# A gated-delta recurrence inside a larger two-block network: one state tile per head with an identity half, and epilogues emitted in more, smaller steps

## The chip, the cores and the metric

One NeuronCore of a Trainium2 chip runs the whole program in one launch. The metric is the device time of one execution in microseconds. The kernel before took 4145.36 us, the median of three runs (4140.95 to 4150.91). All data are float32.

## The reference

The program is a chain of two blocks on one sequence of 1024 tokens with 1024 features. The change lies in the second layer of the first block, in its recurrent branch. What is computed there, cut to the part that matters:

```python
def wkv_scan(r, w, k, v, a, bb, s0, reverse):
    def step(s, inp):
        r_t, w_t, k_t, v_t, a_t, b_t = inp
        sa = jnp.einsum("bhvk,bhk->bhv", s, a_t)
        s = s * w_t[:, :, None, :] + sa[..., None] * b_t[:, :, None, :] + v_t[..., None] * k_t[:, :, None, :]
        return s, jnp.einsum("bhvk,bhk->bhv", s, r_t)
    ...
# rwkv_branch: 8 heads of 64, once forward and once backward (d = 0, 1)
    s_fin, o = wkv_scan(r_h, heads(decay), k_d, v_h, -kk, kk * a_h, init, reverse=(d == 1))
# then: o = outs[0] + outs[1], normalised per head, times lnx_g, plus lnx_b, plus bonus * v, times the gate g
```

A context of 256 tokens is scanned first and gives the states with which the 1024 tokens start. Beside the recurrence the layer has dense projections (`h @ in_o`), a 31-tap convolution with a layer norm (`conformer_branch`) and an output projection (`y @ w_out`). Before this layer come its even neighbour, after it two feed-forward layers, a token mixer with top-k attention and norms.

## The kernel before

**Chunks.** The scan is done in chunks of 64 tokens. Four chunks of a pair of heads in one direction make a *group*; there are 4 head pairs, 2 directions and 5 groups each (group 0 is the context), so 40 groups, numbered n = 0 to 39. Five groups of one pair and direction are a *unit* (u = 0 to 7). The two heads of a pair lie on partitions 0 to 63 and 64 to 127 (`H[0]`, `H[1]`).

**Three stages per group.** `s1` (L660) builds decayed keys, queries and the chunk's triangular matrices and stores them in DRAM (`d_rec`). When all five groups of a unit are there, `elim` (L716) inverts the triangular 32x32 blocks by elimination, one part of the columns on VectorE (tiles `elUV`, `elTV`), the other on GpSimd (`elUP`, `elTP`), reading `elM` from `d_rec` and writing `d_el`; the other stages take them from there as `Tc` (L748). `s2` (L744) then makes from them, in steps, for each chunk the transition matrix Q and an additive matrix C (L777 to 789) and walks the four chunks (L798 to 805): output `o = S q + C`, new state `S = decay * (Q S + S + C)`. The three terms of the state are three matmuls that accumulate in PSUM, two of them by the identity (`mm`, L804); the output has two (L801). Each works on 64 rows and 64 columns of the array, one set for each head. VectorE scales the sum by the decay into the next of four state tiles `SI` (L805).

**Epilogues.** When both directions of a quarter of a head pair are done, `finish` (L810) loads the two outputs (`fok`), adds them on GpSimd (L816), normalises per head with transposes through TensorE (L824, L829, L844) and stores `d_yc`. `cln` (L599) is the same for the convolution branch and stores `d_yd`. Smaller epilogues of the projections are `g` inside `fk` (norm of the keys: ScalarE squares `kq`, L520, TensorE sums them, L523) and `norm` (L535). They are generators that wait in two lists, `later[0]` (projection epilogues and `cln`) and `later[1]` (`finish`).

**The order.** The order on TensorE in this layer is written out by hand: matmuls of the recurrence and of the dense work go through `Pinned`, which keeps them in program order. The main loop (L903 to 932) takes for each n four quarters. In each it first issues dense units until a count that grows by 3.2 per n, later by 2.4, is reached (L908 to 912), then one step of `s1` for the newest groups, one step of `s2` for group m = n - 9, and one step of the walk over the chunks for group m - 1. Elimination of a unit is issued when n is a multiple of 5 (L920). After each dense unit `fin` (L885) appends ready epilogues and calls `tick` (L496), which takes each list's first epilogue one step on:

```python
        for l in later:
            while l and next(l[0],l) is l: l.pop(0)
```

`finish` is taken one step on at once when it is appended (`next` in L888), so its loads and its first two operations are issued, and its first matmul in the `tick` behind that. The last dense work is the output projection `outp` (L854), in four batches; each is issued when the epilogues that it reads have been issued (`fins`, L868), and until then every quarter counts 0.25 of a unit without work. All other engines' instructions are placed by a scheduler which knows priorities: 500 for the recurrence, 200 for the elimination (`EPRIO`), 1000 for epilogues.

## Time and profile before

| | |
|---|---|
| median of three runs | 4145.36 us |
| the profiled execution | 4132.25 us, span of its instructions 4130.5 us |
| TensorE (PE) busy | 3639.1 us, 88% |
| VectorE (DVE) busy | 2384.2 us, 58% |
| ScalarE (ACT) busy | 1474.9 us, 36% |
| GpSimd (POOL) busy | 1370.3 us, 33% |
| TensorE weight loads | 3166.6 us, 77% |
| mean granted TensorE clock | 0.921 of full speed |

The layer with the recurrence runs from about 700 to 2010 us of the span; `s2` starts its first group at 928 us. In the stretch the page shows TensorE busy in six to nine tenths of each slice, where the stages behind it show nine tenths, and the granted clock moves between 0.58 and 1.00. A row of the trace names line, engine, operation and out<-in tiles; a float32 matmul stands there as two instructions.

### The profile page before, as it was taken

The numbers are of one execution on the slowest core, as the hardware profiler recorded it, in microseconds if no ns is written. First come the engines' busy times: TensorE is split into PE (matmuls) and PEld (weight loads), VectorE is DVE, ScalarE is ACT, GpSimd is POOL, SyncE is SP. The second block draws the span as 40 slices with busy tenths as digits, with TensorE's granted clock in tenths as the row PEclk, the third lists the DMA queues.
The fourth block names the chain that finished last, engine by engine and source line by source line (L and its number), as shares of the span: only waits on it lengthen the run. The fifth ranks groups of instructions, "written<-read, shape, count | busy, mean of one in ns | idle before, by whom it ended". The sixth has DMA issues, their size and how long they took to land.

```text
span 4130.5 us, 72373 instructions
## 1 busy us (share of the span) xinstructions
PE 3639.1 (88%) x28552; PEld 3166.6 (77%) x28552; DVE 2384.2 (58%) x4265; ACT 1474.9 (36%) x2581; POOL 1370.3 (33%) x2335
## 2 busy tenths in 40 slices
PE   8999988878786867768679999999999989999997
PEld 6889878767775866646479998876666658999885
DVE  4445331358636635736476665654788666666455
ACT  3233222444432534422232223443565333222333
POOL 3021122246526535624353331111343323333012
PEclk9999999888887887879789999999899999999998
DMA  5453564877675767644322214551231002221554
GB/s 209 154 176 121 166 223 149 258 223 223 212 223 177 225 192 231 188 121 127 112 97 83 84 67 163 179 170 60 75 113 42 21 31 94 78 84 53 205 186 160
DMA packets 422997, 594.52 MB, mean 144 GB/s; under 512 B 106590, under 2 KB 322400, under 8 KB 412928
## 3 DMA queue, kind: packets, MB, share of 16 engines
q1 hardware_dynamic: 422656, 589.88, 44.6%
q8 instruction: 225, 3.69, 0.4%
q14 instruction: 116, 0.95, 0.1%
HBM read 453.45 MB, written 136.07 MB: 143 GB/s over the span
## 4 chain that ended last, share of the span: by engine, by line
PE 58%; DMA 13%; DVE 10%; POOL 6%; issue 6%; ACT 5%; SPq 2%; POOLq 0%; DVEq 0%; ACTq 0%
PE ps L72 13%; PE ps L73 13%; PE ps L74 13%; PE ps L21 10%; DMA wr<-in_f_w 2%; PE ps L1262 2%; PE ps L1250 1%; DVE elUV L738 1%; POOL elTP L737 1%; POOL elUP L738 1%; DVE elTV L737 1%; DMA d_ok<-O 1%; PE ps L1260 1%; DMA raw<-in_in_e 1%; DMA d_xh<-hls 1%
## 5 line engine op out<-in xcount | busy, mean ns | idle before, releaser
L21 PE MATMUL ps<-xq,hi 128*128 128x256 f32 x1632 | 329.4, 302 | 0.0
L72 PE MATMUL ps<-B,ffC 128*128 128x256 f32 x1056 | 298.7, 283 | 5.5 <-DVE ffC L88 2.9
L73 PE MATMUL ps<-B,ffC 128*128 128x256 f32 x1056 | 298.0, 282 | 3.6 <-DVE B L88 3.6
L74 PE MATMUL ps<-B,ffC 128*128 128x256 f32 x1056 | 298.3, 282 | 0.0
L21 PEld LDWEIGHTS ps<-xq,hi 128*128 128x128 f32 x1632 | 280.5, 210 | 3.2 <-issue 2.7
L73 PE MATMUL ps<-w,g 128*128 128x512 f32 x680 | 270.5, 398 | 13.3 <-DVE w L88 12.9
L74 PE MATMUL ps<-w,g 128*128 128x512 f32 x680 | 267.7, 394 | 0.0
L21 PE MATMUL ps<-xq,lo 128*128 128x256 f32 x816 | 258.1, 316 | 1.7 <-DMA xq<-d_xh 1.7
L88 DVE TENSOR_TENSOR w<-wr,w 128x1024 fp32r<-128x1024 f32 x132 | 172.2, 1305 | 138.4 <-ACT w L88 138.0
L72 PE MATMUL ps<-h,lo 128*128 128x320 f32 (+2 forms) x768 | 242.4, 317 | 2.5 <-DVE lo L67 1.7
L73 PE MATMUL ps<-h,hi 128*128 128x320 f32 (+2 forms) x768 | 239.4, 312 | 1.0 <-DVE h L262 1.0
L72 PE MATMUL ps<-w,g 128*128 128x512 f32 x680 | 233.4, 393 | 7.7 <-ACT w L88 4.4
L74 PE MATMUL ps<-h,hi 128*128 128x320 f32 (+2 forms) x768 | 238.9, 311 | 0.0
L67 DVE TENSOR_TENSOR lo<-raw,hi 128x1024 fp32r<-128x1024 f32 (+1 forms) x128 | 159.8, 1249 | 116.1 <-ACT hi L66 115.8
L997 POOL TENSOR_TENSOR ffraw<-ffraw 128x512 f32<-128x512 f32 x44 | 60.1, 1365 | 484.0 <-DVE A L88 484.0
L72 PE MATMUL ps<-B,A 128*128 128x256 f32 x704 | 201.5, 286 | 19.4 <-DVE A L88 18.0
L72 PE MATMUL ps<-B,S 128*128 128x256 f32 x704 | 203.1, 289 | 13.9 <-DVE S L88 13.9
L88 ACT CAST w<-wr 128x1024 fp32r<-128x1024 f32 x132 | 138.6, 1050 | 194.8 <-DMA wr<-in_f_w 111.4
L72 PEld LDWEIGHTS ps<-B,ffC 128*128 128x128 f32 x1056 | 200.0, 189 | 6.4 <-ACT B L88 3.3
L73 PE MATMUL ps<-B,S 128*128 128x256 f32 x704 | 202.6, 288 | 0.2
L73 PEld LDWEIGHTS ps<-B,ffC 128*128 128x128 f32 x1056 | 199.6, 189 | 4.0 <-DVE B L88 4.0
L73 PE MATMUL ps<-B,A 128*128 128x256 f32 x704 | 201.0, 286 | 1.8 <-DVE B L88 1.8
(487 smaller groups left out, 11173.8 us busy)
## 6 DMA issues: line engine op xcount, KB each, us to landing
xq<-d_xh SPq DMA_DIRECT2D x148, 512.0 KB
wr<-in_f_w SPq DMA_DIRECT2D x132, 512.0 KB
ffraw<-in_f_w SPq DMA_DIRECT2D x44, 1024.0 KB
d_rec<-R SPq DMA_DIRECT2D x32, 1024.0 KB
Q<-d_rec SPq DMA_DIRECT2D x32, 1024.0 KB
raw<-in_in_e SPq DMA_DIRECT2D x48, 512.0 KB
d_gg<-ffs SPq DMA_DIRECT2D x88, 256.0 KB
gr<-d_gg SPq DMA_DIRECT2D x44, 384.0 KB
```

Source lines behind the costliest of these rows:

```text
L21: def matmul(s,*a,**k): return s.pin(s.t.matmul(*a,**k))
L67: nc.vector.tensor_tensor(lo[:,:n],raw[:,:n],hi[:,:n],op=ALU.subtract)
L72: first=t.matmul(ps,lt[1],rt[0],start=start,stop=False)
L73: t.matmul(ps,lt[0],rt[1],start=False,stop=False)
L74: t.matmul(ps,lt[0],rt[0],start=False,stop=stop)
L88: s.nc.scalar.copy(hi,src); s.nc.vector.tensor_tensor(lo,src,hi,op=ALU.subtract)
L737: e.tensor_tensor(t,bc(M[:,sr,x:x+1],[80,ns,nj]),bc(U[:,x:x+1,jr],[80,ns,nj]),op=ALU.mult)
L738: e.tensor_tensor(U[:,sr,jr],U[:,sr,jr],t,op=ALU.add)
L997: nc.gpsimd.tensor_tensor(r[:,1],r[:,1],r[:,0],op=ALU.add)
L1250: p=k.ps("at"); nc.tensor.matmul(p[:,:m],q[r,h//2],kT[r,h//2,c0:c0+m],start=True,stop=True)
L1260: for c in range(m): nc.tensor.transpose(p[:,128*c:128*c+128],s[:,128*(c0+c):128*(c0+c)+128],ident)
L1262: for c in range(b+1): nc.tensor.matmul(po3[r,h//2],VT[:,c,64*h:64*h+64],pT[:,c],start=c==0,stop=c==b)
```

## The change

The state tile of each head now is 128 rows high: 64 rows of state and 64 rows of identity, kept in place (two tiles `SI` of [128, 2, 64] in turn, L650 after the change). Q and C no longer are two matrices: one matmul of full width (128 rows, 128 columns) per head and chunk gives both halves of a matrix `Q0` or `Q1`, and the identity that was added by its own matmul is added once by VectorE on the way out of PSUM. A step of the walk then has one matmul of 128 rows and 64 columns per head for the output and one for the state, in place of two and three. VectorE scales the state in two instructions, one per head, where it was one; the copy of `pk` (L765) moves from VectorE to ScalarE; the copies of C leave ScalarE. `finish` is appended without its first step, has an extra `yield` between its loads and its first operations and another ahead of its last matmuls; `g` of `fk` begins with a `yield`, with two buffers of `kq` and `rT`; `cln` has a list of its own; `tick` takes up to two entries of the first list one step on and one of each other list. `outp` counts 6 units for its first batch where it counted 4. The elimination's priority rises from 200 to 600.

```diff
-EPRIO=200
+EPRIO=600
...
-    later=([],[]); fins=set()
+    later=([],[],[]); fins=set()
     def tick():
-        for l in later:
-            while l and next(l[0],l) is l: l.pop(0)
+        for l,m in zip(later,(2,1,1)):
+            j=0
+            while j<m and j<len(l):
+                if next(l[j],l) is l: l.pop(j)
+                else: j+=1
...
-            q=F.tile([128,256],F32,tag="kq",name="kq"+nm)
+            q=F.tile([128,256],F32,tag="kq",bufs=2,name="kq"+nm)
             nc.scalar.activation(q,y,AF.Square,scale=V('k_k')[:,i:i+1])
             def g():
+                yield
...
-                for t in (n//2-4,n//2-3): later[0].append(cln(t))
+                for t in (n//2-4,n//2-3): later[2].append(cln(t))
...
-    NS=4
-    SI=[P.tile([128,64],F32,name="SI%d"%j) for j in range(NS)]
+    NS=2
+    SI=[P.tile([128,2,64],F32,name="SI%d"%j) for j in range(NS)]
+    for j in range(NS):
+        nc.vector.tensor_copy(SI[j][64:128,0],ident[64:128,64:128]); nc.vector.tensor_copy(SI[j][0:64,1],ident[0:64,0:64])
...
-        KV=A0+1; nc.vector.tensor_copy(R[:,:,KV],pk)
+        KV=A0+1; nc.scalar.copy(R[:,:,KV],pk)
...
-            for h in range(2): k.pe.matmul(p[H[h],c,:m],z[h][:,c,ks],R[:,c,T0+h:T0+h+5*m-4:5],start=True,stop=True)
-        nc.scalar.copy(q[:,:,0],p[:,:,0])
-        if isx: nc.vector.tensor_tensor(q[:,:,1],p[:,:,1],R[:,:,AR1],op=ALU.add)
-        p=k.ps("b1").rearrange("p (a b c) -> p a b c",a=4,b=2)
-        for c in range(4):
-            for h in range(2):
-                k.pe.matmul(p[H[h],c,0],R[:,c,T0+h],z[h][:,c,vs],start=True,stop=True)
-                if isx: k.pe.matmul(p[H[h],c,1],z[h][:,c,vs],R[:,c,RS0+h],start=True,stop=True)
-        nc.scalar.copy(C[:,:,:m],p[:,:,:m])
+            for c in range(4): k.pe.matmul(p4[:,c,:m],z[h][:,c],R[:,c,T0+h:T0+h+5*m-4:5],start=True,stop=True)
+            nc.vector.tensor_tensor(q[:,:,0],p4[:,:,0],bc(ident[:,H[h]].unsqueeze(1),[128,4,64]),op=ALU.add)
+            if isx:
+                nc.vector.tensor_tensor(q[H[h],:,1],p4[H[h],:,1],R[H[h],:,AR1],op=ALU.add)
+                nc.scalar.copy(q[H[1-h],:,1],p4[H[1-h],:,1])
...
-                for h in range(2): mm((po3[H[h],c],si[H[h]],q[H[h],c,1]),(po3[H[h],c],I_(h),C[H[h],c,1]))
+                for h in range(2): k.pe.matmul(po3[H[h],c],si[:,h],Q[h][:,c,1],start=True,stop=True)
...
-                for h in range(2): mm((p[H[h]],q[H[h],c,0],si[H[h]]),(p[H[h]],I_(h),si[H[h]]),(p[H[h]],I_(h),C[H[h],c,0]))
-                nc.vector.tensor_scalar(nx,p,PC[:,c],None,op0=ALU.mult)
+                for h in range(2): k.pe.matmul(p[H[h]],Q[h][:,c,0],si[:,h],start=True,stop=True)
+                for h in range(2): nc.vector.tensor_scalar(nx[H[h],h],p[H[h]],PC[H[h],c],None,op0=ALU.mult)
...
     def finish(i,hf):
...
+        yield
+        nc.gpsimd.tensor_tensor(ok[:,0:3:2],ok[:,0:3:2],ok[:,1:4:2],op=ALU.add)
...
         nc.vector.tensor_tensor(dd,dd,bc(rs.unsqueeze(2),[128,4,64]),op=ALU.mult)
         yield
+        yield
...
-                yield 0.01+(n==0)*4
+                yield 0.01+(n==0)*6
...
-                later[1].append(finish(*ready.pop(0)[1:])); next(later[1][-1])
+                later[1].append(finish(*ready.pop(0)[1:]))
```

Over the whole program TensorE has 1440 matmuls fewer (23482 before, 22042 after), VectorE 268 instructions more, ScalarE 24 copies and 3 table loads more. GpSimd has 8 memsets more, the DMA issues are the same in number.

**Place 1, the walk.** TensorE's rows of one step of the walk, both heads (unit 4, group 3; `Q`, `C` and `SI` are the transition, the additive matrix and the state; the first and the last row are the products ahead of the step and behind it; a row stands for one head, the other head's rows read alike and are left out, so that of ten products five are shown). Before:

```order
L21 MATMUL ps1716_17750<-Z0_1_6190,Q4_4_17538 64x64
L21 MATMUL ps1717_17770<-Q4_3_17652,SI0_6197 64x64
L21 MATMUL ps1717_17770<-C4_3_17653,ident_61 64x64
...
L21 MATMUL ps1717_17770<-SI0_6197,Q4_3_17652 64x64
L21 MATMUL ps1717_17770<-SI0_6197,ident_61 64x64
L21 MATMUL ps1717_17770<-C4_3_17653,ident_61 64x64
...
L21 MATMUL ps1718_17791<-R6_3_17525,BKB6_3_17530 128x128
```

After the change, the same step (`Q0`, `Q1` are the matrices of the two heads, the first and the last row the products ahead of it and behind it):

```order
L21 MATMUL ps1726_17199<-Z0_1_6190,Q4_4_16867 64x64
L21 MATMUL ps1727_17219<-Q0_4_3_17130,SI0_6197 64x64
L21 MATMUL ps1727_17219<-Q1_4_3_17139,SI0_6197 64x64
L21 MATMUL ps1727_17219<-SI0_6197,Q0_4_3_17130 64x64
L21 MATMUL ps1727_17219<-SI0_6197,Q1_4_3_17139 64x64
L21 MATMUL ps1728_17235<-R6_3_16854,BKB6_3_16859 128x128
```

Ten matmuls of the step have become four, and none of them works on the identity.

**Place 2, an epilogue's first matmul.** TensorE between the last product of the walk whose output an epilogue reads (unit 3, group 1) and the epilogue's first matmul (`fok`, head pair 1, quarter 3; `xq` is dense work). Before:

```order
L21 MATMUL ps1523_15240<-SI3_6200,ident_61 64x64
L21 MATMUL ps1523_15240<-C3_1_15099,ident_61 64x64
L21 MATMUL ps1559_15517<-xq1563_15523,lo1549_15496 128x256
L21 MATMUL ps1559_15517<-xq1563_15523,hi1549_15495 128x256 x2
...
L21 MATMUL ps1573_15675<-lwc5_3_15290,W2r_5_14225 128x256 x2
L21 MATMUL ps1574_15715<-Tc3_3_15211,Q3_3_15207 32x32 x8
...
L21 MATMUL ps1574_15715<-TU0_6201,X3_3_15219 32x32 x8
L21 MATMUL ps1575_15735<-Q3_2_15480,SI1_6198 64x64
...
L21 MATMUL ps1575_15735<-C3_2_15481,ident_61 64x64
L824 MATMUL ps1569_15648<-fok1_3_15630,BD_6161 128x256
```

After the change:

```order
L21 MATMUL ps1524_14795<-SI1_6198,Q1_3_1_14722 64x64
L21 MATMUL ps1559_15043<-xq1563_15049,lo1549_15022 128x256
L21 MATMUL ps1559_15043<-xq1563_15049,hi1549_15021 128x256 x2
...
L21 MATMUL ps1571_15166<-lwc5_3_14828,W2r_5_13833 128x256 x2
L21 MATMUL ps1572_15206<-Tc3_3_14766,Q3_3_14762 32x32 x8
...
L21 MATMUL ps1560_15044<-xq1561_15045,lo1555_15034 128x256
...
L21 MATMUL ps1573_15226<-Q0_3_2_15095,SI0_6197 64x64
...
L21 MATMUL ps1560_15044<-xq1563_15049,lo1555_15034 128x256
L827 MATMUL ps1584_15370<-fok1_3_15155,BD_6161 128x256
```

The epilogue's first matmul stands 56 rows behind the product before, 24 dense matmuls among them, and 85 rows behind it after, 52 of them dense matmuls. Over the 16 epilogues there are 0 to 72 dense matmuls in between before, and 0 to 267 after; in the epilogues of head pairs 0 and 1 24 to 72 before and 52 to 267 after.

**Place 3, the stretch ahead of the output projection.** TensorE between the first product with the inverse (`Tc`) of group 4 and that of the next unit's group 0, on both sides of the first work of the output projection (`yo`). Before:

```order
L21 MATMUL ps1716_17750<-Tc4_4_17542,Q4_4_17538 32x32 x8
L21 MATMUL ps1716_17750<-Z0_0_6189,Q4_4_17538 64x64
...
L21 MATMUL ps1717_17770<-C4_3_17653,ident_61 64x64
L21 MATMUL ps1720_17824<-hi1699_17456,yo1_1691_17435 128x512
L21 MATMUL ps1720_17824<-lo1699_17457,yo0_1691_17434 128x512
L21 MATMUL ps1720_17824<-hi1699_17456,yo0_1691_17434 128x512
...
L21 MATMUL ps1732_17977<-lwc7_0_17789,W2r_7_17784 128x256 x2
L21 MATMUL ps1733_18017<-Tc5_0_17739,Q5_0_17735 32x32 x8
```

After the change:

```order
L21 MATMUL ps1726_17199<-Tc4_4_16871,Q4_4_16867 32x32 x8
L21 MATMUL ps1726_17199<-Z0_0_6189,Q4_4_16867 64x64
...
L21 MATMUL ps1732_17288<-Q4_4_16867,TU0_6203 128x128 x4
L21 MATMUL ps1727_17219<-Q0_4_3_17130,SI0_6197 64x64
...
L21 MATMUL ps1735_17329<-lwc7_0_17233,W2r_7_17228 128x256 x2
L21 MATMUL ps1736_17369<-Tc5_0_17188,Q5_0_17184 32x32 x8
```

Before, the output projection began between the two products, and 24 of its matmuls stood there; two groups ahead of it (unit 4, groups 2 and 3) had no dense work. Now there is none between them, it starts behind the second, and three groups (unit 4, groups 3 and 4, unit 5, group 0) have no dense work.

## Rows read from the trace of the kernel before

**Rows 1.** Page, busy time of each engine, and the clock over 40 slices of the span.

```profile
PE 3639.1 (88%) x28552; PEld 3166.6 (77%) x28552; DVE 2384.2 (58%) x4265; ACT 1474.9 (36%) x2581; POOL 1370.3 (33%) x2335
...
PEclk9999999888887887879789999999899999999998
```

**Rows 2.** Stretches: start:end, length, busy (instructions) of PE, PEld, DVE, ACT, POOL; clock; DMA.

```profile
938.00:1685.00 747.00, 579.49 (x7373) 522.03 (x7374) 435.78 (x1048) 297.10 (x668) 373.44 (x743) 0.82 0.70 212
1590.00:1611.00 21.00, 20.69 (x294) 18.91 (x294) 19.33 (x54) 12.03 (x29) 19.69 (x46) 1.00 0.68 179
...
1732.00:1795.00 63.00, 28.05 (x277) 22.48 (x274) 28.75 (x63) 20.77 (x41) 29.95 (x61) 0.58 0.44 116
```

**Rows 3.** Waits of PE, 700 to 2060: us in total, times, longest.

```profile
PE ps L824 <- DVE fok L822: 76.4, 14, 10.5
PE ps L523 <- ACT kq L520: 56.1, 10, 15.7
PE ps L844 <- DVE fd L841: 33.7, 6, 15.7
...
PE ps L21 <- DVE Z L775: 25.6, 14, 5.9
PE ps L21 <- DVE yo L88: 18.9, 2, 12.6
...
PE ps L21 <- DVE SI L805: 8.2, 7, 3.1
...
PE ps L607 <- DMA cin<-d_C: 6.0, 1, 6.0
```

**Rows 4.** Timeline of PE, one step of the walk: start, length, operation, tile, count.

```profile
1000.31 1.16 PE L21 MATMUL ps<-Q,TU 128*128 128x128 f32 x8
1001.40 0.34 PE L21 MATMUL ps<-Q,SI 64*64 64x64 f32 x4
...
1001.68 0.28 PE L21 MATMUL ps<-SI,Q 64*64 64x64 f32 x2
...
1002.29 0.38 PE L21 MATMUL ps<-xq,lo 128*128 128x256 f32 x1
```

**Rows 5.** Timeline of PE, products for Q and C of one group.

```profile
1005.33 1.09 PE L21 MATMUL ps<-Q,Z 128*64 128x128 f32 x16
1006.25 0.34 PE L21 MATMUL ps<-Z,Q 128*64 128x64 f32 x4
1006.37 0.34 PE L21 MATMUL ps<-Q,Z 128*64 128x64 f32 x4
...
1007.33 0.34 PE L21 MATMUL ps<-Q,SI 64*64 64x64 f32 x4
```

**Rows 6.** Timeline, all engines: one epilogue from the output copy to its first matmul.

```profile
1149.81 0.36 ACT L809 COPY O<-ps 128x256 f32<-128x256 f32 x1
...
1158.76 0.34 SPq L814 DMA_DIRECT2D fok<-d_ok  x1
...
1164.85 1.26 POOL L816 TENSOR_TENSOR fok<-fok 128x512 f32<-128x512 f32 x1 [7.87 <-DMA fok<-d_ok]
...
1166.68 1.22 PE L824 MATMUL ps<-fok,BD 128*128 128x256 f32 x2 [8.76 <-DVE fok L822]
```

**Rows 7.** Groups of DVE by form, 700 to 2060: busy, mean ns | idle before.

```profile
L805 DVE TENSOR_SCALAR SI<-ps,PC 128x64 f32<-128x64 f32 x152 | 42.1, 277 | 30.4 <-PE ps L21 29.0
...
L783 DVE TENSOR_TENSOR Q<-ps,Q 128x256 f32<-128x256 f32 x32 | 13.4, 419 | 39.4 <-ACT Q L782 39.4
```

**Rows 8.** Timeline of SP, elimination of units 3 and 5: load of elM, load of Tc.

```profile
1235.20 0.97 SPq L722 DMA_DIRECT2D elM<-d_rec  x2
...
1366.37 1.21 SPq L748 DMA_DIRECT2D Tc<-d_el  x2
...
1562.38 1.15 SPq L722 DMA_DIRECT2D elM<-d_rec  x2
...
1651.46 0.65 SPq L748 DMA_DIRECT2D Tc<-d_el  x1
```

More of the change, by code (lines that the diff above doesn't have):

```diff
@@ L624, in zdc @@
             if n%4==0 and n>4:
-                for t in (n//2-4,n//2-3): later[0].append(cln(t))
-        for t in (6,7): later[0].append(cln(t))
+                for t in (n//2-4,n//2-3): later[2].append(cln(t))
+        for t in (6,7): later[2].append(cln(t))
     w0h=P.tile([128,8],F32,name="w0h"); a0h=P.tile([128,8],F32,name="a0h"); omka=P.tile([128,4],F32,name="omka")
@@ L645, in layer1 @@
     for j in range(NZ):
-        for h in range(2): nc.gpsimd.memset(Z[j][h][H[1-h],:,64:128],0.0)
-    NS=4
-    SI=[P.tile([128,64],F32,name="SI%d"%j) for j in range(NS)]
+        nc.gpsimd.memset(Z[j][0][64:128,:,0:64],0.0); nc.gpsimd.memset(Z[j][1][0:64,:,64:128],0.0)
+    NS=2
+    SI=[P.tile([128,2,64],F32,name="SI%d"%j) for j in range(NS)]
+    for j in range(NS):
+        nc.vector.tensor_copy(SI[j][64:128,0],ident[64:128,64:128]); nc.vector.tensor_copy(SI[j][0:64,1],ident[0:64,0:64])
     TU=[P.tile([128,4,128],F32,name="TU%d"%j) for j in range(2)]
@@ L752, in s2 @@
         for q in range(4): nc.gpsimd.tensor_scalar(t[32*q:32*q+32,:,32*q:32*q+32],Tc[32*q:32*q+32],1.0,1.0,op0=ALU.mult,op1=ALU.mult)
-        vs,ks=slice(0,64),slice(64,128)
-        for h in range(2): nc.scalar.copy(z[h][H[1-h],:,vs],vv[H[1-h]])
+        vs=[slice(64,128),slice(0,64)]; ks=[slice(0,64),slice(64,128)]
+        nc.scalar.copy(z[0][H[1],:,vs[0]],vv[H[1]]); nc.scalar.copy(z[1][H[0],:,vs[1]],vv[H[0]])
         X=T.tile([128,4,32],F32,tag="X",name="X"+nm)
@@ L762, in s2 @@
         for c in range(4):
-            for h in range(2): k.pe.matmul(pk[H[h],c],R[H[1-h],c,A0+h],z[h][H[1-h],c,vs],start=True,stop=True)
+            for h in range(2): k.pe.matmul(pk[H[h],c],R[H[1-h],c,A0+h],z[h][H[1-h],c,vs[h]],start=True,stop=True)
         for h in range(2): nc.scalar.copy(X[sr(h)],px[sr(h)])
-        KV=A0+1; nc.vector.tensor_copy(R[:,:,KV],pk)
+        KV=A0+1; nc.scalar.copy(R[:,:,KV],pk)
         yield
@@ L780, in s2 @@
-        for c in range(4):
-            for h in range(2): k.pe.matmul(p[H[h],c,:m],z[h][:,c,ks],R[:,c,T0+h:T0+h+5*m-4:5],start=True,stop=True)
-        nc.scalar.copy(q[:,:,0],p[:,:,0])
-        if isx: nc.vector.tensor_tensor(q[:,:,1],p[:,:,1],R[:,:,AR1],op=ALU.add)
-        p=k.ps("b1").rearrange("p (a b c) -> p a b c",a=4,b=2)
-        for c in range(4):
-            for h in range(2):
-                k.pe.matmul(p[H[h],c,0],R[:,c,T0+h],z[h][:,c,vs],start=True,stop=True)
-                if isx: k.pe.matmul(p[H[h],c,1],z[h][:,c,vs],R[:,c,RS0+h],start=True,stop=True)
@@ L789, in s2 @@
-        nc.scalar.copy(C[:,:,:m],p[:,:,:m])
+        Q=[]
+        for h in range(2):
+            q=T.tile([128,4,2,64],F32,tag="Q%d"%h,name="Q%d_%s"%(h,nm)); Q.append(q)
+            p=k.ps("b%d"%h); p4=p.rearrange("p (a b c) -> p a b c",a=4,b=2); m=2 if isx else 1
+            for c in range(4): k.pe.matmul(p4[:,c,:m],z[h][:,c],R[:,c,T0+h:T0+h+5*m-4:5],start=True,stop=True)
[3 more added lines that the diff above has]
+                nc.scalar.copy(q[H[1-h],:,1],p4[H[1-h],:,1])
@@ L790, in s2 @@
         yield
-        if g==0: nc.gpsimd.memset(SI[cnt['si']%NS],0.0)
+        if g==0:
+            si=SI[cnt['si']%NS]
+            for h in range(2): nc.gpsimd.memset(si[H[h],h],0.0)
         po=k.ps("o"); po3=po[:,:256].rearrange("p (a b) -> p a b",a=4); ps=po[:,256:]
-        def mm(*a):
-            for j,(o,l,r) in enumerate(a):
-                k.pe.matmul(o,l,r,start=j==0,stop=j==len(a)-1)
         for m,c in enumerate(range(4) if d==0 else range(3,-1,-1)):
-            si=SI[cnt['si']%NS]; nx=SI[(cnt['si']+1)%NS]; cnt['si']+=1; I_=lambda h: ident[H[h],H[h]]
+            si=SI[cnt['si']%NS]; nx=SI[(cnt['si']+1)%NS]; cnt['si']+=1
@@ L935, in layer1 @@
         y=next(act,None); fin(99)
-        if y is None and not (ready or later[0] or later[1]): break
+        if y is None and not (ready or any(later)): break
     es.close()
```

12 lines of the change are left out of this document (5 added, 7 removed).

## The prediction

> **What bounds the kernel now.** I read the page first: TensorE is busy for 88% of the span, no other engine for more than 58%, and the clock string is lowest in the middle [rows 1]. So the time is TensorE's, and what can be won lies where it stands or runs slowly. Then the stretches [rows 2]: 938 to 1685 us is the recurrence beside dense work, 25 groups in 747 us, and TensorE is busy for 579 of them at a mean clock of 0.82. VectorE is busy for 436 (58%), GpSimd for 373 (50%). One group there needs 21.0 us when nothing disturbs it (1590 to 1611: TensorE busy for 20.7, clock 1.00). 25 of those are 525 us; the other 222 are some 160 us of idle TensorE and some 62 us of longer busy time, most of it at the lower of the clock's two levels (1.2 and 2.4 GHz). The worst piece, 1732 to 1795, is busy for 28 of 63 us at a clock of 0.58. Then the waits [rows 3]: three places hold 166 us, the first matmul of an epilogue (L824, 76.4), the sum of the key norms (L523, 56.1) and an epilogue's last transposes (L844, 33.7). The waits inside the recurrence are smaller (25.6 behind copies of Z, 8.2 behind the state). TensorE's order is fixed, so in each of these waits work stands ready behind the waiting matmul.
>
> **The sum is made against the profiled execution, 4132 us.** It is 13 us under the median of 4145; I add these at the end.
>
> **(a) The walk.** Of 160 steps (40 groups, four chunks) 120 have output and state, 32 (context groups) only the state, 8 (last chunk of a unit) only the output. A full step takes 0.89 us from its first start to the start of the next form (1001.40 to 1002.29): 0.28 output, 0.61 state with the change of form behind it [rows 4]. The new form, 128 rows by 64 columns with 64 moving, exists already: four such instructions, two heads with two each, start 0.12 us apart, and the eight fours with the change of form behind them take 1.08 us, so that the change costs about 0.14 [rows 5]. The new step is 0.12 + 0.12 + 0.14 = 0.38 us. Saved: 120 x 0.51 + 32 x (0.61 - 0.26) + 8 x (0.42 - 0.26) = 61 + 11 + 1 = 74 us. The products for Q and C took 0.92 + 1.08 = 2.00 us per group [rows 5]. Now they are 16 instructions of full width; eight of that size take 1.09 us [rows 4], 0.11 each and some 0.2 at the ends, so 2.0 again: nothing. Where TensorE waits a little later the saving becomes waiting; 22% of the stretch is idle, so I count three quarters, **-55 us** (ends: half, -37, where another engine sets the pace, and -74).
>
> By the Trainium skill, TensorEngine Tiling (Array Packing), "Tiling Modes", different tiles load and multiply independently of each other. The old step would then be bounded by one head's five products, ten instructions at half of 0.12 us, 0.58 us with 0.14 behind; the saving would be 0.34 us a full step and this term some 50 us, with three quarters -37. The row shows 0.89, not 0.72: in the hand-written order the tiles overlap only in part, and I take the row.
>
> **(b) The epilogue's first matmul (L824).** Its chain from the copy of the output to the matmul took 16.9 us (1149.81 to 1166.68), two DMA passes through DRAM with 8.9 and 6.1 us in it, and TensorE stood for 8.8 of them [rows 6]. A unit of 24 dense matmuls is 3.0 us (1002.29 to 1005.33) [rows 4, 5]. Before, 24 to 72 of them lay in between in head pairs 0 and 1, 3 to 9 us; now 52 to 267, 7 to 34 us, and the recurrence's own products besides (place 2). Three epilogues, the first of pairs 0 to 2, stay a few us short, and the last pair's have no dense work at all. Of 76.4 us 60 go. **(c) Key norms (L523).** One `yield` is one unit, 3 us, less at a block's first and last chunk. Ten waits with a mean of 5.6 us and a longest of 15.7 [rows 3] lose at most 3 each: 28 go. The long ones, which wait for a congested ScalarE or VectorE, stay in part. **(d) L844.** One more unit lies ahead of it: 28 of 33.7 go. **(e) `cln` by itself.** It no longer stands behind other epilogues: the wait of 12.6 us of an output batch and the 6.0 us behind the load of `cin` [rows 3] go, 18 us. Together **-134 us**.
>
> **What of this comes back.** VectorE gets 152 more state scalings of 0.277 us, 42 us, and a net of 112 more additions for Q0 and Q1 of at most 0.419 us, 47 us [rows 7]; copies of Z, and of the product that goes to ScalarE, come out even in columns or better. ScalarE's exchange is even by columns too. So VectorE gets up to 89 us in 40 groups, 2.2 us per group, and goes from 58% to some 70% in shorter groups. It is not the bound on the mean, but beside an elimination it is nearly full (19.3 of 21 us in the stretch from 1590) [rows 2]. A wait that is gone then shows the next one: the copies of Z, the state, R. Ends: none, and two thirds of the 134; I take **+50**, nearer to the lower end since the three waits were chains over DRAM and GpSimd, beside which VectorE was idle. DMA issues are the same in number; the loads of an epilogue leave SP where they did, at its first step, so that nothing new queues behind them. In the walk VectorE's part of the chain grows by 0.28 us and TensorE's falls by 0.51; without cover it is shorter than it was.
>
> **(f) New waits.** Place 3: one group more without dense work, which has products for some 11 us (21.0 less 3.2 units of 3.0) and chains of copies between them: +8 (0 to 15). The first output batch now follows directly on the last epilogue that it reads, and so does the fourth; store, load and two casts are uncovered. By the two known waits of this kind (12.6, the longest, and 6.3, the total less the longest) [rows 3] I take +6 and +10. The elimination of unit 5 took 89 us from its load to the load of its result (1562.38 to 1651.46) [rows 8]; of its 3.75 groups three now have no dense work, at 14 us each and 20 for the rest, 62 us, so TensorE may wait for up to 27; I take +14, and +4 for the other units. Together **+42** (20 to 60). Table loads, three more on ScalarE, lie beside other work.
>
> **(g) Clock.** Of the 62 us of longer busy time I give back a third, **-20**, since half of the idle time stays (ends 0 and -62). By the Trainium skill, TensorE: Matmul & The Clock Gate, "Why this matters for your kernels", a clock that fell in a gap stays down only for gaps; if all were closed, all 62 would return and the total were 42 lower. The row agrees in kind: 1.00 in the undisturbed group, 0.58 in the worst.
>
> **Sum.** -55 - 134 + 50 + 42 - 20 = -117: 4132 - 117 = 4015, and with the 13 us **4028 us**. The rest of the program keeps its instructions in a slightly different interleaving; I count nothing for that.
>
> **Rivals.**
> - *The gaps close.* Nothing comes back, few new waits, more clock: -74 - 134 + 20 - 40 = -228, 3917 us. For it: in undisturbed groups no engine limits TensorE. Against it: VectorE and GpSimd at 92% beside an elimination [rows 2]. Up to 3980 us: 18%.
> - *The waits only move.* Half of (a), two thirds of the stalls back, 60 us of new waits, no clock: -37 - 134 + 90 + 60 = -21, 4124 us. For it: key norms waited behind busy engines, and one unit of cover doesn't change what those do. Against it: the largest wait was a DRAM chain. From 4090 to 4137 us: 13%. That the change does not do what it says would end here too; against that speaks the order, in which the products are gone and the epilogues stand farther apart.
> - *Slower: elimination becomes the bound.* It starts when a unit's last group is stored and must be done 3.75 groups later, on VectorE and GpSimd, with VectorE 8 us fuller in that time. If it binds in every unit, a unit takes its turnaround plus 1.25 groups of 30 us; five groups take 149 us today (747 / 25 x 5), so it decides from a turnaround of 112 us on. Unit 3 had 131 us (1235.20 to 1366.37), unit 5 89 [rows 8]. At 131 in all six units beside dense work: 131 + 37 - 149 = 19 us each, +114, less some 20 of gain behind them: 4239 us. Against it: unit 3's was long since its groups were long, and the raised priority works the other way. 5%.
>
> **How the numbers follow.** About 0.2%, 8 us, is what can be told from no change here: 4137 to 4154 us is "same". The forecast with its near misses (3980 to 4090) has 60%, the first rival 18%, the second 13%, no change 4%, slower 5%. So faster 0.91, same 0.04, slower 0.05. The range takes the low end near the first rival and the high end at the second: 3920 to 4120 us.
>
> **What would show it.** In the profile after: products of state and Q at 128 rows, 0.38 us a step; the wait at the epilogue's first matmul under 20 us in all, at the key norms near 30, at the last transposes under 10; VectorE busy for 60 to 90 us more; a wait for `Tc` of unit 5, and for `yo` some 10 us longer than now; a mean clock over 0.93. I am wrong if the waits behind VectorE (Z, state, R) grow by more than 90 us, if `Tc` waits in most units, or if TensorE's busy time in the layer falls by less than 40 us.

## The result, and the profile after

The changed kernel took 4093.76 us, the median of four runs (4080.21 to 4095.44), beside 4145.68 us of the kernel before: a ratio of 0.9867 (95% interval 0.9843 to 0.9892), some 55 us less by the ratio and 52 by the medians. A second series gave 0.9868 (0.9846 to 0.9890). The profiled execution has a span of 4093.4 us, 37 us under that of before. The forecast was a gain of 117 us; the direction held, the size was less than half.

The page after, busy time of each engine and the clock over 40 slices [rows 1]:

```profile
PE 3595.4 (88%) x25672; PEld 3119.6 (76%) x25672; DVE 2471.2 (60%) x4533; ACT 1481.3 (36%) x2608; POOL 1359.7 (33%) x2343
...
PEclk9999999887887887798699999999899989999998
```

Stretches of before that were not shown yet, in the columns of [rows 2]: the whole layer, from the first product for the decays to the last epilogue's last transposes, and VectorE's part of the eliminations of units 1 and 3:

```profile
703.60:2030.50 1326.90, 1013.62 (x12242) 895.85 (x12241) 725.20 (x1723) 505.90 (x1118) 604.54 (x1268) 0.83 0.65 197
955.00:1046.00 91.00, 74.93 (x984) 68.39 (x982) 78.29 (x192) 34.84 (x84) 64.25 (x100) 0.88 0.73 230
1245.00:1354.00 109.00, 72.30 (x870) 66.25 (x871) 77.89 (x169) 31.11 (x74) 68.27 (x95) 0.75 0.58 181
```

The same after, and the stretch that answers to the first of [rows 2]:

```profile
707.60:1991.80 1284.20, 971.74 (x9362) 850.30 (x9360) 812.27 (x1987) 513.02 (x1145) 591.41 (x1269) 0.82 0.67 202
938.00:1685.00 747.00, 564.37 (x5678) 505.63 (x5677) 504.17 (x1240) 320.65 (x718) 384.74 (x789) 0.80 0.72 220
953.00:1064.00 111.00, 82.94 (x864) 75.19 (x863) 93.20 (x224) 43.37 (x104) 60.91 (x103) 0.78 0.66 207
1243.00:1369.00 126.00, 89.97 (x868) 80.05 (x864) 109.33 (x254) 48.16 (x113) 77.32 (x120) 0.81 0.66 212
```

The layer is 42.7 us shorter (1326.9 to 1284.2), and all of that is TensorE's busy time (1013.6 to 971.7). Its idle time is what it was, 313 us before and 312.5 after, and its clock is a little lower (0.83 and 0.82). To part work from clock I multiplied each matmul record's time, from its start to the next one's, by the granted clock at that moment: the busy time comes to 883 us of full clock before and 820 after. So 63 us of work went; the lower of the two levels (1.2 and 2.4 GHz) cost 130 us before and 151 after, and took 21 of them back. The size of that last step is not firm: a second profile of the changed kernel has 823 us of work, 319 us of idle time and 137 us lost by the clock. In neither did the clock give anything back. VectorE has 87 us more, and its part of two eliminations now takes 111 and 126 us where it took 91 and 112.

The waits of TensorE after, in the window of [rows 3]:

```profile
PE ps L557 <- DVE yv L517: 58.6, 9, 14.0
PE ps L22 <- DVE R L710: 50.8, 30, 6.6
PE ps L21 <- DVE Z L782: 34.4, 15, 5.5
PE ps L21 <- DMA Tc<-d_el: 25.8, 3, 13.0
PE ps L21 <- DVE yo L88: 24.0, 3, 14.8
PE ps L848 <- DVE fd L844: 22.3, 4, 8.8
PE ps L21 <- DVE TU L775: 13.9, 8, 4.6
PE ps L21 <- DVE SI L807: 11.0, 7, 3.9
...
PE ps L827 <- DVE fok L825: 7.7, 3, 4.3
...
PE ps L827 <- issue: 4.2, 1, 4.2
```

The three large waits fell from 166 to some 35 us, where the forecast left 50: an epilogue's first matmul 76.4 to 11.9 (7.7 and 4.2), the key norms 56.1 to about 1, the last transposes 33.7 to 22.3, which were to fall under 10. In their place stand the transposes of the values (yv, 8.3 before), the masks of R (25.8 before), Z (25.6), Tc (4.0) and TU: all but Tc end on VectorE, and Tc is the elimination, a part of which is VectorE's. The second profile has the same list (56.8, 54.6, 36.2, 26.6 and 15.1 us).

The walk is what it was taken for. A step from [rows 4], after:

```profile
1163.73 1.95 PE L21 MATMUL ps<-Q,Z 128*128 128x128 f32 x16
1165.61 0.34 PE L21 MATMUL ps<-Q,SI 128*64 128x64 f32 x4
1165.78 0.29 PE L21 MATMUL ps<-SI,Q 128*64 128x64 f32 x4
1165.99 0.38 PE L21 MATMUL ps<-xq,lo 128*128 128x256 f32 x1
```

1165.61 to 1165.99 is 0.38 us, the forecast's number; the products for Q0 and Q1 take 1.88 us (2.0 forecast). VectorE's part is also as large as was said [rows 7]; its groups by form, after:

```profile
L807 DVE TENSOR_SCALAR SI<-ps,PC 64x64 f32<-64x64 f32 x304 | 85.8, 282 | 51.3 <-PE ps L21 45.2
...
L790 DVE TENSOR_TENSOR Q<-ps,ident 128x256 f32<-128x256 f32 x80 | 33.5, 418 | 38.2 <-PE ps L21 36.4
L782 DVE COPY Z<-ps 64x256 f32<-64x256 f32 x80 | 29.9, 411 | 2.7 <-ACT Z L781 1.9
L792 DVE TENSOR_TENSOR Q<-ps,Q 64x256 f32<-64x256 f32 x64 | 26.7, 417 | 0.5
```

Beside which work these instructions fall is seen in VectorE's own timeline inside the elimination of unit 3 (elTV and elUV are its steps, C the taps of the convolution):

```profile
1354.09 0.17 DVE L744 TENSOR_TENSOR elUV<-elUV,elTV 80x24 f32<-80x24 f32 x1
1354.29 0.75 DVE L782 COPY Z<-ps 64x256 f32<-64x256 f32 x2
1354.96 1.26 DVE L596 SCALAR_TENSOR_TENSOR C<-H,vecs,C 128x448 f32<-128x448 f32 x2
1356.15 0.17 DVE L743 TENSOR_TENSOR elTV<-elM,elUV 80x20 f32<-80x20 f32 x1
1356.24 0.41 DVE L844 TENSOR_TENSOR fd<-fd,rsy 128x256 f32<-128x256 f32 x1
1356.58 1.13 DVE L596 SCALAR_TENSOR_TENSOR C<-H,vecs,C 128x384 f32<-128x384 f32 x2
1357.63 0.16 DVE L744 TENSOR_TENSOR elUV<-elUV,elTV 80x20 f32<-80x20 f32 x1
1357.72 0.41 DVE L790 TENSOR_TENSOR Q<-ps,ident 128x256 f32<-128x256 f32 x1
```

There is no idle bracket (a mark of idle time before a row) in it. Each step of the elimination takes 0.17 us, needs the one before it, and follows it here after 1.5 to 2.1 us, since an epilogue, the recurrence and the convolution stand in between. All 62 steps of unit 3 took 126 us, 20 of them their own. The end of that chain, first on SP (load of elM, load of Tc, [rows 8]) and then on TensorE:

```profile
1234.10 4.85 SPq L728 DMA_DIRECT2D elM<-d_rec  x4
...
1377.91 4.48 SPq L754 DMA_DIRECT2D Tc<-d_el  x3
```

```profile
1380.65 0.64 PE L21 MATMUL ps<-Tc,Q 32*32 32x32 f32 x16 [13.00 <-DMA Tc<-d_el]
```

Unit 3's turnaround, from the one load to the other, was 131 us, and TensorE did not wait for it; it is 144 now, and TensorE stands for 13 us. VectorE's part is by far the last to end in units 1 and 3, where the convolution runs beside it: in unit 3 it ended at 1369 us and GpSimd's at 1304 (before: 1357 and 1309).

### The profile page after: what moved, and what is told of

It is laid out like the page before. It is cut to its first block, busy times and chain, and to the rows that moved or that the text cites. A ratio compares the mean times of both kernels' runs of the same rounds, so it can differ in the third digit from the quotient of the medians.

```text
span 4093.4 us, 66944 instructions
## 1 busy us (share of the span) xinstructions
PE 3595.4 (88%) x25672; PEld 3119.6 (76%) x25672; DVE 2471.2 (60%) x4533; ACT 1481.3 (36%) x2608; POOL 1359.7 (33%) x2343
## 4 chain that ended last, share of the span: by engine, by line
PE 58%; DVE 12%; DMA 10%; issue 7%; POOL 7%; ACT 4%; SPq 1%; POOLq 0%; DVEq 0%; ACTq 0%
PE ps L72 13%; PE ps L73 13%; PE ps L74 13%; PE ps L21 9%; PE ps L1266 2%; PE ps L1254 1%; DMA wr<-in_f_w 1%; DMA d_xh<-hls 1%; DVE elUV L744 1%; DVE elTV L743 1%; POOL elTP L743 1%; DMA raw<-in_in_e 1%; PE ps L1264 1%; POOL elUP L744 1%; DVE C L596 1%
## 5 line engine op out<-in xcount | busy, mean ns | idle before, releaser
L21 PE MATMUL ps<-xq,hi 128*128 128x256 f32 x1632 | 338.1, 307 | 0.0
L73 PE MATMUL ps<-w,g 128*128 128x512 f32 x680 | 269.7, 397 | 11.9 <-DVE w L88 11.2
```

The lines of the kernel that those rows point to most:

```text
L21: def matmul(s,*a,**k): return s.pin(s.t.matmul(*a,**k))
L73: t.matmul(ps,lt[0],rt[1],start=False,stop=False)
```

## The experiments

Every ratio is to the kernel before in the same series, with its 95% interval; "us" is the ratio's difference from 1 times 4145. W is the kernel before with the state tile alone, E the one with the epilogues' part alone. A filler is matmuls added to give TensorE work; few taps leaves out most of the convolution; NCUT 32 puts the elimination wholly on GpSimd; the value step is one more `yield` ahead of the transposes of the values; priority is the elimination's. Each is shown below.

| run | ratio (interval) | us |
|---|---|---|
| W | 1.0013 (1.0000 to 1.0026) | +5 |
| W, filler behind the scaling | 1.0290 (1.0268 to 1.0312) | +120 |
| W, filler ahead | 1.0056 (1.0038 to 1.0074) | +23 |
| W, half the scaling on ScalarE | 0.9986 (0.9974 to 0.9998) | -6 |
| before, few taps | 0.9905 (0.9886 to 0.9923) | -39 |
| W, few taps | 0.9856 (0.9837 to 0.9875) | -60 |
| before, NCUT 32 | 0.9921 (0.9905 to 0.9938) | -33 |
| W, NCUT 32 | 0.9869 (0.9851 to 0.9887) | -54 |
| E | 0.9916 (0.9897 to 0.9935) | -35 |
| E, value step | 0.9861 (0.9843 to 0.9879) | -58 |
| before, priority 600 | 1.0015 (1.0000 to 1.0030) | +6 |
| **the change** | 0.9867 (0.9843 to 0.9892) | -55 |
| the change, second series | 0.9868 (0.9846 to 0.9890) | -55 |
| priority back to 200 (W and E) | 0.9848 (0.9830 to 0.9865) | -63 |
| value step | 0.9845 (0.9827 to 0.9863) | -64 |
| 4 units ahead of the output | 0.9922 (0.9905 to 0.9939) | -32 |
| NCUT 32 | 0.9693 (0.9672 to 0.9713) | -127 |
| NCUT 32, priority 200, value step | 0.9672 (0.9649 to 0.9695) | -136 |
| the same, half the scaling on ScalarE | 0.9685 (0.9663 to 0.9708) | -131 |

**The walk alone.** The kernel before with the diff's lines from the state tiles to `finish` (SI, Z, the copy of pk, Q0, Q1, the walk), the rest as before.

> The kernel before with the change of the state tile alone: Q0/Q1, four products a step, the copy of pk on ScalarE; epilogues, lists and priority as before. By the forecast's own terms: the walk's TensorE time falls by about 72 us at full clock, three quarters of it reach the end, VectorE gives some 25 us back: 4115 us. New theory (work taken out between waits that stay becomes idle time and a lower clock): the three waits at L824, L523, L844 stay within 20 us of their 166, TensorE's idle time in the layer grows by 30 us or more, the clock between 938 and 1685 us falls under 0.82, and the time is 4130 us (4118 to 4146). Rival (the walk's time counts in full): 4075 us.

It took 4148.25 us, no gain. The waits, the idle time and the clock came as the new theory has them (the three waits 147 us); the time lies just outside its 4118 to 4146. Its layer and waits:

```profile
703.60:2046.20 1342.60, 978.03 (x9362) 853.92 (x9361) 809.23 (x1987) 508.87 (x1142) 593.86 (x1276) 0.80 0.65 194
```

```profile
PE ps L822 <- DVE fok L820: 65.0, 11, 12.5
PE ps L22 <- DVE R L706: 48.9, 30, 6.4
PE ps L523 <- ACT kq L520: 46.5, 8, 16.3
PE ps L21 <- DVE Z L778: 42.2, 18, 5.2
```

TensorE's work falls by 64 us of full clock, as in the whole change; idle time rises from 313 to 365 us, and the lower clock costs 158 us where it cost 130. VectorE has 84 us more in the layer. Two causes can do this: TensorE's saving lies beside other work, or VectorE's new work takes it back. The next runs part them.

**The same TensorE time as before, the rest of the walk.** Two fillers. The first, behind VectorE's scaling, was badly placed; the diff shows the second.

```diff
             if isx:
-                for h in range(2): k.pe.matmul(po3[H[h],c],si[:,h],Q[h][:,c,1],start=True,stop=True)
+                for _ in range(5):
+                    for h in range(2): k.pe.matmul(po3[H[h],c],si[:,h],Q[h][:,c,1],start=True,stop=True)
```

> The walk alone, and behind each step's state products the output products of both heads four times more (the same values into the same places), so that a step takes TensorE again about what the old one took; VectorE's new work and all waits stay as in the walk alone. Theory (what the walk saves on TensorE was cover for the other engines' chains, so it turned into idle time, 51 us, and a lower clock, 28 us): TensorE's busy time at full clock rises by 55 to 65 us, its idle time falls by 35 us or more, the clock rises, and the time stays within 12 us of the walk alone, 4148 us. Rival (TensorE's own time is the bound, and the walk brought nothing because VectorE's new work cost 64 us elsewhere): the filler is paid in full, 4200 us.

```profile
PE ps L21 <- DVE SI L803: 170.8, 99, 9.7
```

This one measures a wait that it made itself (170.8 us, 8.4 in the walk alone) and says nothing on the question. With the filler ahead, as in the diff:

> The walk alone, with the output products of both heads issued five times in place of once, ahead of the state's products (the filler of the run before stood behind VectorE's scaling in the program and waited for it, 171 us in 99 waits, so that it told nothing). The step takes TensorE about 0.5 us more, some 61 us at full clock, and nothing else changes. Theory (TensorE's time in the walk lay beside other engines' work): idle time falls by 35 us or more against the walk alone (364), and the time is within 15 us of 4148. Rival (TensorE's time counts in full, and VectorE's new work cost what the walk saved): 4195 us or more.

```profile
705.30:2055.00 1349.70, 1013.80 (x11410) 895.42 (x11409) 801.89 (x1987) 513.18 (x1144) 595.71 (x1276) 0.83 0.64 193
```

It took 4170.01 us: neither number was met. TensorE does 61 us more of full clock (820 to 881) for 18 us of time (1.0013 to 1.0056), and idle time falls by 29. So a microsecond of TensorE's work in the walk is worth some 0.3 us (0.14 to 0.44 by the intervals). At that price the walk's 64 were worth some 19, and as the walk alone gave nothing, its work on VectorE cost as much or a little more.

**Part of the scaling on ScalarE.**

```diff
-                for h in range(2): nc.vector.tensor_scalar(nx[H[h],h],p[H[h]],PC[H[h],c],None,op0=ALU.mult)
+                nc.vector.tensor_scalar(nx[H[0],0],p[H[0]],PC[H[0],c],None,op0=ALU.mult)
+                nc.scalar.activation(nx[H[1],1],p[H[1]],AF.Identity,scale=PC[H[1],c])
```

> The walk alone, with the state scaling of the second head on ScalarE in place of VectorE: 152 instructions of 0.28 us, some 42 of the 70 us that the walk adds to VectorE, go to ScalarE, which is busy for 40%. TensorE's work is that of the walk alone. The filler run puts the walk's saving on TensorE at 22 us, the walk alone measured 0: so VectorE's new work costs some 25 us. Theory: 42 of 70 us of it give 15 us: 4133 us (4122 to 4140). Rival (ScalarE's queue makes the state wait, as it is in line behind casts of 1 us): SI's wait on TensorE grows by more than 15 us and the time is 4148 us or more.

The ratio went from 1.0013 to 0.9986, 11 us, with TensorE's work unchanged: VectorE has 52 us less in the layer (809 to 757), of the 84 that the walk had added, and that gives back about half of the 24 that were missing.

**VectorE relieved by other means.** The convolution cut to 3 of its 31 taps, in the kernel before and in the walk alone (28 taps are left out):

```diff
-            for a in range(1,16):
+            for a in range(1,2):
```

> The kernel before with 3 of the convolution's 31 taps (the other 28, 112 instructions and some 85 us on VectorE between 942 and 1366 us, are left out). For comparison with the next run. Theory (VectorE is the bound where the convolution and an elimination fall together): 4120 us (4100 to 4135), from shorter waits of the epilogues and key norms alone, as Tc was no wait here.

> The walk alone, with 3 of the convolution's 31 taps as in the run before it. Theory (the walk's 70 us more on VectorE fall on an engine that is 70 to 95% busy while an elimination runs, and cost what TensorE saves): with 85 us less on VectorE the walk's gain shows: 20 us or more under the kernel before without these taps, some 4090 us, and the waits for Tc (25.8 us) under 8. Rival (the walk brings nothing for a reason of TensorE's own, its fixed order and its clock): the two differ by less than 8 us, as with all taps.

They took 4109.42 and 4088.10 us: without these taps the walk gains 21, and its wait for Tc is gone from the list. The 112 instructions had taken 80 us, but VectorE's busy time in the layer falls by 59 (725 to 666) and 62 us (809 to 747), for which the kernel before gains 39 and the walk 65. These taps lie beside the eliminations of units 1 and 3. GpSimd gains as well: by the profile its same instructions take 565 us in place of 605, and 564 in place of 594 in the walk, so that VectorE's own time is not all that the taps give back. Then the elimination wholly on GpSimd, all else as it was:

```diff
-NCUT=28
+NCUT=32
```

> The changed kernel with the elimination wholly on GpSimd (NCUT 32 in place of 28), so that VectorE is rid of 62 instructions a unit, some 120 us in all, and GpSimd's part grows by about a sixth (45 to 52 us). Theory (VectorE is the bound beside an elimination): R and Z together fall from 85 to under 60 us, VectorE's end no longer sets Tc in units 1 and 3, and the time falls by 20 us or more: 4070 us. Rival (GpSimd is as full, 88 to 92% beside an elimination, and becomes the bound): Tc waits in more units and the time is 4094 us or more.

> The kernel before with the elimination wholly on GpSimd (NCUT 32). Theory (VectorE's fullness beside an elimination took the change's gain): before, VectorE had more room and Tc was waited for once (4.0 us), so the same step brings less here than the 70 us in the changed kernel: 4115 us (4095 to 4130), and with VectorE free the whole change is worth 80 us or more (4024 against this). Rival (the step is worth the same in either kernel, and the change's 52 us have nothing to do with VectorE): 4075 us, a difference of 52 again.

> The walk alone, with the elimination wholly on GpSimd. Theory: the walk's gain, which was nothing with NCUT 28, shows when VectorE has room: 25 us or more under the kernel before with NCUT 32, some 4085 us, TensorE's idle time in the layer 40 us or more under the 364 of the walk alone. Rival (TensorE's fixed order, not VectorE, turns the walk's saving into idle time): within 8 us of the kernel before with NCUT 32.

They took 4024.18, 4113.26 and 4090.99 us. The layer of the kernel before, of the walk alone and of the changed kernel with it, and the waits of the last:

```profile
706.00:2008.30 1302.30, 1015.00 (x12243) 898.38 (x12241) 607.60 (x1213) 507.24 (x1112) 643.97 (x1332) 0.84 0.65 200
705.60:1984.90 1279.30, 962.27 (x9362) 842.10 (x9361) 696.55 (x1477) 507.19 (x1134) 641.10 (x1340) 0.81 0.66 204
707.90:1923.30 1215.40, 955.59 (x9362) 837.44 (x9360) 696.52 (x1477) 511.83 (x1137) 636.79 (x1332) 0.84 0.69 214
```

```profile
PE ps L557 <- DVE yv L517: 49.2, 9, 12.1
PE ps L21 <- DVE Z L782: 41.5, 19, 5.6
PE ps L22 <- DVE R L710: 35.0, 29, 6.5
```

And its turnaround of unit 3:

```profile
1208.62 4.45 SPq L728 DMA_DIRECT2D elM<-d_rec  x4
...
1290.26 2.30 SPq L754 DMA_DIRECT2D Tc<-d_el  x1
```

The same 113 to 118 us off VectorE bring 33 us before, 59 with the walk and 72 with the whole change, where VectorE had been busy for 55, 60 and 63% of the layer: the fuller VectorE is, the more. With VectorE relieved the walk is worth 21 us (25 expected) where it was worth -5, and the change 94 where it was worth 55. R and Z together fell from 85 to 77 only, not under the 60 expected; what went is the idle time as a whole (312 to 260), Tc (25.8 to 5.3) and unit 3's turnaround, 82 us in place of 144. NCUT 32 does two things: it frees VectorE, and it ends the eliminations of units 1 and 3 sooner, since GpSimd is through with all 32 columns (63 us in unit 3) before VectorE was with its four (126). It also gives GpSimd 39 to 47 us more. These runs don't part the two; few taps leaves the elimination divided as it was, and there VectorE's relief pays as well.

**The epilogues alone, and their value step.** E is all of the diff outside the walk and the priority. The step:

```diff
             def g():
+                yield
                 p=k.ps(tags[2]); p3=p[:,:256].rearrange("p (a b) -> p a b",a=4)
```

> The kernel before with the epilogues' part alone (three lists, two entries of the first list per step, the extra steps, two buffers of kq and rT, 6 units ahead of the first output batch); state tile, walk and priority as before. The forecast's terms (b) to (e) less half of the new waits: -134 + 42 = some -90, 4055 us. New theory: L824, L523 and L844 lose 120 us or more, but the sum over the value transposes (yv) grows by 40 to 50 us and the masks of R by 10 to 20: 4095 us (4080 to 4110). If the two parts add, this run and the walk alone together give the 52 us of the whole change; if each uses up the other's room, together more than 52.

> The epilogues' part alone, with one more step ahead of the transposes of yv (its wait there was 69.4 us in 9 times, where it was 8.3 before). Theory (the rest of the epilogues' gain, 36 of a forecast 92, went into this one wait): yv under 10 us, the time 4070 us (4055 to 4085). Rival (the value transposes wait for a VectorE and ScalarE that are late anyway, so that the next reader waits instead): the idle time falls by less than 20 us under the 283 of the epilogues alone, the time is 4095 us or more.

E took 4108.73 us, inside its bounds, and with the step 4079.80: the second misses its 4070 and lies in its bounds, while idle time falls from 283 to 250. In the waits of E a large part of the gain of three places comes back at one, yv; R hardly grew (25.8 to 26.4), against the 10 to 20 us expected:

```profile
PE ps L557 <- DVE yv L517: 69.4, 9, 15.4
PE ps L22 <- DVE R L708: 26.4, 23, 4.4
```

The rows show how. Before, the key norms' sum came first behind the dense units and waited; the values, one unit later, found their tile ready:

```profile
1127.29 1.01 PE L523 MATMUL ps<-BO,kq 128*128 128x2 f32 x4 [9.07 <-ACT kq L520]
...
1131.86 1.12 PE L553 MATMUL ps<-ident,yv 64*64 64x64 f32 x16
```

After, the values come first, since the key norms' new step passes the turn to the list's second entry, and a similar lateness is met there:

```profile
1144.55 1.12 PE L557 MATMUL ps<-ident,yv 64*64 64x64 f32 x16 [8.17 <-DVE yv L517]
...
1145.97 0.85 PE L527 MATMUL ps<-BO,kq 128*128 128x2 f32 x4
```

In E the step is worth 23 us. In the whole change the same edit, and the priority put back, gave:

> The changed kernel with one more step ahead of the transposes of the values (yv), as the key norms have it. Theory: since two entries of the first list go on together, the transposes of yv are issued one dense unit earlier than before, and the key norms' wait (56.1 to under 2 us) came back there (8.3 to 58.6 us); with the step yv waits for under 15 us, key norms still under 5, and the time falls by 25 to 45 us: 4060 us. Rival (both only show that ScalarE and VectorE are late with the dense work's results, so the wait goes to the next reader): yv falls, other waits grow by as much, and the time stays within 10 us of 4094.

> The changed kernel with the elimination's priority at 200 again. Theory: raised over the recurrence (500), the elimination's 60 instructions stand ahead of the masks of R on VectorE, and R's wait grew from 25.8 to 50.8 us by that; with 200 it falls under 35 us and the time by 10 to 25 us (4075 us), unless the wait for Tc (25.8 us) grows by as much. Rival: R waits longer because VectorE has 77 us more of its own work; R stays over 45 us and the time within 8 us of 4094.

Their intervals overlap with the change's own, so that 4076.61 and 4078.63 us can't be told from it, and the value step's 4060 was missed; that is why the change was timed again, and the priority alone was put into the kernel before:

> The changed kernel once more, with more executions beside those of the kernel before: its ratio of 0.9867 had an interval of 0.9843 to 0.9892, which overlaps with those of the priority put back (0.9848) and of the value step (0.9845). If those two edits are real the ratio is 0.987 or more; at 0.985 or less neither can be told from nothing.

> The kernel before with the elimination's priority alone at 600. Theory (ahead of the recurrence on VectorE and GpSimd it makes the masks of R wait): R's wait grows from 25.8 us to over 33 and the time by 5 to 15 us: ratio 1.001 to 1.004. Rival (before, VectorE has room, so that order does not matter): 0.999 to 1.001.

R's wait does go from 50.8 to 33.3 us with the priority back. But in the kernel before with priority 600 it is 22.9 us, not over the 33 expected, and in W, with 200, it is 48.9; so the priority is not shown to be what makes R wait. What it costs stays open: between nothing and some 20 us. In the value step's run Tc waits for 47.1 us in place of 25.8, so that there the relieved wait showed the elimination behind it.

**The output projection's start** (`yield 0.01+(n==0)*4` in place of 6):

> The changed kernel with 4 units counted ahead of the first output batch, as before, in place of 6. Theory (place 3 costs what was forecast, since three groups have no dense work and the batch waits for its own loads): the batch begins some 0.8 groups earlier, the wait of yo grows by up to 10 us, Tc's in unit 5 (7.8 us) falls, together within 10 us of 4094. Rival (the longer stretch without dense work is what ate the gain): 4075 us or less.

Slower, 4103.38 us, 0.9922 beside 0.9867: by the ratios, which allow for the series, both expectations were wrong, and the run is some 20 us slower. In this trace all of that lies behind the layer, which itself is 9 us shorter than in the change's. The rest of the program is 16 us longer with the same 12240 instructions on TensorE and the same idle time (141 and 139 us); the difference is the clock, whose lower level costs 58 us there, 40 in the change's trace and 49 in its second. How the start of the output projection would bring that about is not shown.

**A version that beats both:** the change with NCUT 32, priority 200 and the value step, and then half of the scaling on ScalarE as well.

> The changed kernel with three edits together: the elimination wholly on GpSimd, its priority at 200, one more step ahead of the transposes of yv. Alone they brought 70, 15 and 17 us. If they take different waits: 3992 us (3980 to 4005). If the priority no longer matters (VectorE holds no elimination) and only the step adds: 4007 us. Rival (all three relieve the same VectorE queue): 4024 us, within 8.

> The changed kernel with elimination on GpSimd, priority 200 and the value step, and the state scaling of the second head on ScalarE. Theory (VectorE still sets the pace: 480 of 747 us, and the waits for Z and R are left): another 8 to 15 us, 3998 us. Rival (with the elimination gone VectorE is no bound, and ScalarE's queue makes SI wait): 4011 us or more.

4011.03 and 4010.13 us, against 4024.18 for NCUT 32 alone; the three can't be told apart. With the elimination off VectorE, less work on it brings nothing more that these runs can tell.

## Why the prediction was wrong in size

**What bounds the kernel.** "So the time is TensorE's" was the first wrong step. TensorE is the busiest engine, but its work in the walk is worth 0.3 us per us (filler), and VectorE's 0.28 before, 0.5 with the walk and 0.6 with the whole change by NCUT 32 (the elimination's earlier end and GpSimd's added work are in it), and 0.7 before and about 1 with the walk by the taps, which lie beside two eliminations. By the Trainium skill, Perfetto Trace Analysis, "Identifying the Most-Contended Engine", one improves the engine with the highest occupancy first. Here the measurement differs for the layer: in W TensorE at 73% of it (978.0 of 1342.6; 64% by its weight loads, which the page prefers) was worth less than VectorE at 60%.

**(a) The walk, -55.** 0.38 us a step came out as said, and 63 to 64 us of the 74 in all. What failed is "I count three quarters": by the filler's price some 19 us, a quarter of the 74, would have been right.

**What comes back, +50.** The work on VectorE was sized well (87 us in the layer, up to 89 forecast). Its price was not: "It is not the bound on the mean" looked at 58%, where VectorE is busy for 72 to 95% of its part of an elimination before and for 84 to 94% after (in units 1 and 3 78.29 of 91 and 77.89 of 109, then 93.20 of 111 and 109.33 of 126). The new work made these parts longer: 407 us in units 1 to 7 before, 461 after. I had that number, 19.3 of 21 us, and took it for a short stretch. The end of this range, two thirds of 134 or 90, was nearer.

**(b) to (e), -134, and (f), +42.** (b) gave 64 of a forecast 60, (d) 11 of 28, and (c), forecast 28, took away 55 at the key norms and gave 50 back at yv, 5 in all: I did not follow the second entry that the new `tick` pulls forward. Of (e)'s 18 some 11 went: the second output batch waits for 5.4 us, behind a cast, in place of 12.6, and what waits for cin went from 9.5 to 5.9. Alone this part gave 35 us where these terms say 92; the value step is 23 of the missing 57. (f)'s size was right: the first output batch waits for 14.8 us in place of 6.3 (+6 forecast), the fourth for 8.7 (+10), and Tc for 22 us more (18 forecast), but half of Tc's 25.8 in unit 3 and 7.8 in unit 5, where 14 were forecast.

**(g) The clock, -20.** Nothing came back: the clock's loss went from 130 to 151 us, 137 in the second profile. That work left while the idle time stayed fits it, and so does the filler, with which W lost 133 us in place of 158. But with the epilogues alone (idle 283) the loss is 128 and with the value step (idle 250) 137; so the sum of the idle time does not set it, and the cause of its size stays open. By the Trainium skill, TensorE: Matmul & The Clock Gate, "Why this matters for your kernels", gaps are what brings the clock down; the runs agree with that only in part, as these pairs show.

**The parts don't add.** Walk, epilogues and priority alone sum to -24 (+5, -35, +6); together -55. The expectation of E let them add up or bring more apart than together; it was the opposite. Where the epilogues' waits are gone the walk is worth 28 us (E to both parts), where they stand nothing.

**The rivals.** "The waits only move" (-21 against the profile, 13%) names what happened better than the forecast, the time lies between. "Elimination becomes the bound" has its mechanism right in units 1, 3 and 5 (waits of 5.0, 13.0 and 7.8 us), but not in every unit; in 1 and 3 VectorE's part ends last, in 5 GpSimd's (1617 us, VectorE's 1599). **In sum.** Between the 117 forecast and the profiles' 37 lie 80 us: 41 of clock (21 lost, 20 forecast as gain), 11 of work that TensorE kept (63 in place of 74), 22 of idle time (forecast 23 less: -134, +50, +42 and the 19 of the walk that become waiting; measured 1) and 6 outside the layer, 4 ahead of it and 2 behind. By the second profile (40 us under before) the 77 are some 27 of clock, 14 of work, 29 of idle time and 8 outside. So the largest share is idle time or clock, by the execution taken. The medians differ by 52, since the profiled execution of before was 13 us under its median.

## What to carry to other kernels

Before work is moved from the busiest engine to another, look at the other's share in each stretch, not its mean, and for a chain of short dependent steps in its line: each new instruction that stands between two of them makes the whole chain end later. A wait that goes can come back at the next reader of results that are as late, so follow the order of the readers. A filler on one engine and a relief of another tell which of them the time belongs to, if the relief does nothing else.

## What was not expected of the hardware

Steps of elimination of some 0.3 us (20 us for 62) came round every 2.0 us on the mean on a VectorE that was busy for 87% of the time, so that an eighth of an elimination's columns (4 of 32) set the end of the whole (VectorE's part ended at 1369 us, GpSimd's at 1304). When VectorE did less (few taps), GpSimd's same 1268 instructions took 39 us less by the profile. And behind the layer TensorE's same instructions, with nearly the same idle time, lost 40, 49 and 58 us by the clock in three executions, 40 and 49 in two of one kernel.
